# Six plain hidden tiles instead of four, two squares' sums moved between engines, and a later column sum

## The chip, the cores and the metric

One core of a Trainium2 chip runs the whole program. The metric is the device time of one execution in microseconds (us); a smaller number is better. The kernel before took 2752.27 us in the median of 3 runs (2752.18 to 2753.72).

## What is computed

Two stacks of two layers each, over 512 tokens of width 1024, in float32. The parts that the change touches are the two normalizations and the second stack's feed forward:

```python
def swiglu(h, w_gate_up, w_down):
    g, u = jnp.split(h @ w_gate_up, 2, axis=-1)      # hidden width 2816 = 22 tiles of 128
    return (jax.nn.silu(g) * u) @ w_down

# end of the first stack, then the start of the second
x = rmsnorm(x, norm_f)
h = rmsnorm_2(x, norm_mix_g[0])
...
mem_n = rmsnorm_2(mem, mem_norm_g[layer])            # mem: 256 tokens of width 1024
x = x + memory_cross_attention(rmsnorm_2(x, norm_xattn_g[layer]), mem_n, ...)
x = x + swiglu(rmsnorm_2(x, norm_ffn_g[layer]), ffn_w_gate_up[layer], ffn_w_down[layer])
```

## The kernel before

**Layout and arithmetic.** The state `x` stays in SBUF as 8 tiles of 128 features by 512 tokens. Every float32 matrix product is made of three matmuls (`mm3`, lines 225 to 227): each operand is split into a high and a low part, and high by high, high by low and low by high are summed in PSUM. Weights come by DMA on SP's queue (`_load`), are split by ScalarE (line 132) and VectorE (line 133), and at most `HL` = 4 split weight tiles are held ahead.

**Order of the work.** The program order on every engine is written out by hand. After each group of 24 matmuls, `tick` (line 200) does four things in this order: it splits weights for what comes next (`pump`), evacuates the PSUM result, runs what was put off, and lets each background generator do one step (`step`, line 177). So a generator advances one `yield` per tick, and what it issues stands in its engine's queue behind the weights and the evacuation of that tick.

**The second stack's feed forward** (`ffn`, line 1069, with `conv=False`; called twice). The 22 hidden tiles are taken in pairs, in the parts that `FPARTS` and `FPARTS_END` list (lines 437 and 438); after each part its down projection follows (`fd`). A pair is made in one of two ways:

- *plain*, for tiles below `PLAIN[1]`: two weight chunks `fa` and `fv`, 2 output tiles each, 8 features tiles deep, so 2 x 2 x 8 x 3 = 96 matmuls of 512 columns, on the input `xh`, `xl`. VectorE multiplies by `Rb` (line 1148), ScalarE applies Silu (line 1087), GpSimd multiplies by `Rb` again (line 1089), VectorE multiplies the two halves (line 1152), and ScalarE and VectorE split the result (lines 237 and 238).
- *by seven products* (`spair`, line 1092): the 2 by 2 block product is done with 7 block products instead of 8, each `product` (line 1054, matmul at line 1065) being 2 x 4 x 3 = 24 matmuls of 256 columns, so 168 for a pair. It needs sums of weight blocks (`schunks`, VectorE adds at line 327) and sums of blocks of the input, `self.A`.

`self.A` is made by the generator `factors` (line 995), which starts in the background after the first pair of `fa` tiles. It takes the 8 tiles of `x` two at a time (`j` = 0 to 3): one step computes `xa`, `xb` and four sums on VectorE (lines 1022 to 1028), the next step splits the sums of the pair before (`put`, ScalarE lines 1008 and 1011, VectorE lines 1009 and 1012). With the first step there are two steps per `j`, and the tenth step sets `self.ready`; four more steps make the factors `12` and `22`. Where the first pair by seven products begins, the code waits for it in program order:

```python
if f == plain:
    while not self.ready:
        self.step()
    self.xh = self.xl = None
```

The tiles of 128 x 512 come from one pool of `NT` = 45 buffers, beside 11 or 13 more for the factors (`ft`, line 1047).

**The end of the first stack.** `norm_tile` (line 543) splits each new tile of `x` and adds its squares up. Squares are made by ScalarE (lines 535 and 537). The running sums are kept by GpSimd for tiles 1 to 4 and by VectorE for tiles 5 to 7 (`dve`, line 547; the add is line 541). At the end of the first stack there are two sets of sums (`ngain2` is given there and nowhere else), since the final norm of the first stack and the first norm of the second are taken together. `even` (line 1294) then starts with `mem_k`: after its first 24 matmuls `norm_gen` (line 587) puts the column sums on TensorE (`colsum`, line 567, matmul at line 575).

**Memory's norm.** `mem_norm` (line 1226) is a generator in the background of the first stack's second feed forward. In one step it issues the squares of 8 tiles on ScalarE and 7 adds on GpSimd, then yields twice, then puts the column sum on TensorE.

Of the kernel before, what the change touches and what calls it, by code (L numbers as in the profile page):

```python
# [14 lines left out]
KT = 8  # L15
# [296 lines left out]
def wchunk(name, w, r0, kc, c0, nc_=256, split=whole):  # L312
    per = 1024 // nc_
    raws = [block(w, r0 + k * P, min(per, kc - k), c0, nc_) for k in range(0, kc, per)]
    return chunk(name, raws, [unit(r["kc"], nc_, split, (i,)) for i, r in enumerate(raws)])


def schunks(name, w, c1, c2):


    b = [block(w, r, 4, c, 256) for r, c in ((0, c1), (0, c2), (512, c2), (512, c1))]

    b11, b12, b22, b21 = b
    box = {}

    def add(c, to, x, y):
        c.nc.vector.tensor_tensor(to, x, y, op=ADD)

    def sum0(c, r):

        box["t"] = c.pf.tile([P, 1024], F32, tag="t0", bufs=1, name=c.nm("t0")).rearrange("p (k c) -> p k c", k=4)
        add(c, box["t"], r[0], r[1])

    def sum1(c, r):

        add(c, r[0], r[0], r[1])

    def sum2(c, r):

        add(c, r[0], r[0], r[1])  # L340

    def post5(c, r):

        add(c, r[0], r[0], r[1])

    def temp(c, hi, lo, raws):
        c.put(hi, lo, box.pop("t"))


    u = [dict(unit(4, 256, whole, (b11,), 0), pre=sum0, praws=(b11, b12)),  # L350
         dict(unit(4, 256, temp, (b11,), 0), pre=sum1, praws=(b12, b22)),
         dict(unit(4, 256, whole, (b11,), 0), pre=sum2, praws=(b11, b12)),
         unit(4, 256, whole, (b22,), 1),
         dict(unit(4, 256, whole, (b21, b11), 1, 1), post=post5, praws=(b21, b11)),
         unit(4, 256, whole, (b12,), 1),
         unit(4, 256, whole, (b21,), 1)]
    out = [chunk(name, [], [x]) for x in u]
    out[0]["raws"] = b
    return out
# [77 lines left out]
FPARTS = ((0, 6), (6, 12), (12, 16), (16, 22))  # L437
FPARTS_END = ((0, 6), (6, 12), (12, 18), (18, 22))

PLAIN = (22, 4)  # L440


def ffn_plan(wu, wd, b, end=False):
    pl, late, first = [], [], []
    pairs = {f: schunks("fs", wu, 2816 + 128 * f, 128 * f) for f in range(PLAIN[b], 22, 2)}
    parts = FPARTS_END if end else FPARTS
    for f0, f1 in parts:
        for f in range(f0, f1, 2):
            if f < PLAIN[b]:
                pl.append(wchunk("fa", wu, 0, 8, 128 * f))  # L450
# [13 lines left out]
        for i in range(2):  # L464
            for f in range(f0, f1, 2):
                pl.append(chunk("fd", [block(wd, 128 * f, 2, 512 * i, 512)], [unit(2, 512)]))
                if i == 0 and f == f0:
                    pl += late
                    late = []
                    if f1 - f0 == 4 and f1 >= PLAIN[b]:  # L470
                        first = pairs[f1][:1]
# [4 lines left out]
class Kern(Ctx):  # L476
# [66 lines left out]
    def norm_tile(self, j):  # L543

        g = self.ngain(j)
        self.xh[j], self.xl[j] = self.split(self.x[j], "x", scale=g)
        dve = j >= KT - 3
        self.sumsq(self.x[j], 0, dve=dve)
        if self.ngain2 is not None:
            self.sumsq(self.x[j], 1, scale=self.ngain2(j), dve=dve)  # L550
# [518 lines left out]
    def ffn(self, l, after, conv):  # L1069
# [3 lines left out]
        last = None  # L1073
        plain = PLAIN[0 if conv else 1]

# [150 lines left out]
    def mem_norm(self):  # L1226

        nc = self.nc
        mem = self.mem_load()
        for _ in range(6):  # L1230
            yield
        save, self.sqs = self.sqs, [[], []]
        for j in range(KT):
            self.sumsq(mem[:, j], 0)
        sq, self.sqs = self.sqs[0], save
        yield
        yield
        v = self.colsum(sq, 2, D)
        r = self.rsqrt(v, 2)
        yield  # L1240
        ps = self.rows(r, 2)
        self.mr = self.pc.tile([P, 2], F32, tag="mr", name="mr")
        nc.vector.tensor_copy(self.mr, r)
        self.mRb = self.pc.tile([P, 256], F32, tag="mRb", name="mRb")
        nc.scalar.copy(self.mRb, ps)
        yield from self.mem_split(0, mem)
# [876 lines left out]
```

## Time and profile before

| what | value |
| --- | --- |
| median of 3 runs | 2752.27 us |
| the profiled execution | 2754.49 us |
| its span, first to last instruction | 2752.5 us |
| mean granted TensorE clock in it | 0.990 |
| TensorE matmul busy | 2694.3 us (98%) |
| VectorE busy | 1652.9 us (60%) |
| ScalarE busy | 1106.1 us (40%) |
| GpSimd busy | 265.4 us (10%) |

The profiled execution is 2.2 us above the median. Matmul durations in the rows overlap each other (a row's 0.39 us is its latency), so a matmul's price is taken from start to start. PE is TensorE, DVE is VectorE, ACT is ScalarE, POOL is GpSimd; L575 is line 575. An arrow `<-` behind idle time names what ended it.

### The profile page before, as it was taken

What the parts mean: (1) busy time and instruction counts of PE and PEld (TensorE: products, weight loads), DVE (VectorE), ACT (ScalarE), POOL (GpSimd) and SP (SyncE); (2) the same over time, 40 slices, a digit from 0 to 9 for tenths busy, and PEclk for the clock granted to TensorE, in tenths of its full rate; (3) what the DMA queues carried; (4) which work ended last, traced back from release to release, by engine and by line L of the source; (5) the groups of instructions that cost most, each with busy time, mean ns of one, the idle gap of its engine ahead of it and who ended that gap; (6) DMA issues with size and microseconds to landing.
All of it is one profiled execution on the core that took longest, in us unless ns stands there. A gap on an engine that the chain in (4) does not pass through costs nothing.

```text
span 2752.5 us, 36388 instructions
## 1 busy us (share of the span) xinstructions
PE 2694.3 (98%) x14606; PEld 2307.3 (84%) x14606; DVE 1652.9 (60%) x2446; ACT 1106.1 (40%) x1668; POOL 265.4 (10%) x337
## 2 busy tenths in 40 slices
PE   8999999999999999999999998999999999989997
PEld 7888888888878888788888887899988888879997
DVE  5644654455455475555566567676766656677666
ACT  4353332233345334332343354443443535444334
POOL 1110200001011011010021201000011001100001
PEclk9999999999999999999999999999999999999999
DMA  5232323332323223332323332242232113223331
GB/s 190 62 93 77 92 92 100 101 99 92 115 63 93 73 89 100 108 100 85 104 81 119 108 99 66 86 127 94 89 93 84 54 47 107 92 77 108 93 100 54
DMA packets 236424, 254.77 MB, mean 93 GB/s; under 512 B 19904, under 2 KB 212672, under 8 KB 235616
## 3 DMA queue, kind: packets, MB, share of 16 engines
q1 hardware_dynamic: 233808, 245.70, 29.1%
q0 software_dynamic: 1440, 5.97, 0.6%
q8 instruction: 114, 1.87, 0.3%
q10 hardware_dynamic: 1008, 0.80, 0.1%
q14 instruction: 54, 0.44, 0.1%
HBM read 248.20 MB, written 2.10 MB: 91 GB/s over the span
## 4 chain that ended last, share of the span: by engine, by line
PE 91%; DVE 5%; ACT 2%; issue 1%; POOL 0%; DMA 0%; ACTq 0%; POOLq 0%; SPq 0%; DVEq 0%
PE ps L225 23%; PE ps L227 23%; PE ps L226 23%; PE ps L1065 13%; PE ps L964 1%; DVE lo L133 1%; PE ps L1740 1%; PE ps L800 1%; PE ps L575 1%; PE ps L1466 0%; PE ps L979 0%; PE ps L890 0%; PE ps L584 0%; ACT hi L132 0%; PE ps L1875 0%
## 5 line engine op out<-in xcount | busy, mean ns | idle before, releaser
L133 DVE TENSOR_TENSOR lo<-raw,hi 128x1024 fp32r<-128x1024 f32 (+3 forms) x519 | 610.3, 1201 | 268.4 <-ACT hi L132 265.4
L225 PE MATMUL ps<-xh,hi 128*128 128x512 f32 x1648 | 649.7, 394 | 7.7 <-ACT hi L132 7.7
L227 PE MATMUL ps<-xh,lo 128*128 128x512 f32 x1648 | 643.7, 391 | 0.7 <-DVE lo L133 0.7
L226 PE MATMUL ps<-xl,hi 128*128 128x512 f32 x1648 | 643.3, 390 | 0.0
L132 ACT ACTIVATE hi<-raw 128x1024 fp32r<-128x1024 f32 (+3 forms) x519 | 509.4, 1012 | 302.8 <-PE ps L226 236.2
L225 PEld LDWEIGHTS ps<-xh,hi 128*128 128x128 f32 x1648 | 310.6, 188 | 73.4 <-ACT hi L132 7.7
L227 PEld LDWEIGHTS ps<-xh,lo 128*128 128x128 f32 x1648 | 310.3, 188 | 67.2 <-DVE lo L133 1.9
L226 PEld LDWEIGHTS ps<-xl,hi 128*128 128x128 f32 x1648 | 310.7, 189 | 63.1 <-issue 0.2
L1065 PE MATMUL ps<-Ah,hi 128*128 128x256 f32 x1008 | 289.1, 287 | 14.1 <-ACT Ah L1008 13.1
L1065 PE MATMUL ps<-Al,hi 128*128 128x256 f32 x1008 | 288.4, 286 | 8.3 <-DVE Al L1009 8.3
L1065 PE MATMUL ps<-Ah,lo 128*128 128x256 f32 x1008 | 287.2, 285 | 0.0
L225 PE MATMUL ps<-acth,hi 128*128 128x512 f32 (+1 forms) x736 | 280.5, 381 | 2.2 <-ACT acth L237 2.2
L226 PE MATMUL ps<-actl,hi 128*128 128x512 f32 (+1 forms) x736 | 280.7, 381 | 0.6 <-DVE actl L238 0.6
L227 PE MATMUL ps<-acth,lo 128*128 128x512 f32 (+1 forms) x736 | 280.2, 381 | 0.0
L660 DVE TENSOR_TENSOR x<-ps,x 128x512 f32<-128x512 f32 x168 | 114.5, 687 | 161.4 <-PE ps L227 161.0
L1065 PEld LDWEIGHTS ps<-Ah,hi 128*128 128x128 f32 x1008 | 195.6, 194 | 16.8 <-ACT Ah L1008 13.9
L1065 PEld LDWEIGHTS ps<-Al,hi 128*128 128x128 f32 x1008 | 195.4, 194 | 10.5 <-DVE Al L1009 9.9
L1065 PEld LDWEIGHTS ps<-Ah,lo 128*128 128x128 f32 x1008 | 195.7, 194 | 0.0
L225 PEld LDWEIGHTS ps<-acth,hi 128*128 128x128 f32 x736 | 138.9, 189 | 28.6 <-ACT acth L237 2.6
L226 PEld LDWEIGHTS ps<-actl,hi 128*128 128x128 f32 x736 | 138.8, 189 | 27.0 <-DVE actl L238 1.3
L227 PEld LDWEIGHTS ps<-acth,lo 128*128 128x128 f32 x736 | 138.9, 189 | 26.4
L541 POOL TENSOR_TENSOR sq<-sq,sq 128x512 f32<-128x512 f32 (+1 forms) x53 | 69.6, 1319 | 695.5 <-ACT sq L535 695.0
(400 smaller groups left out, 3800.5 us busy)
## 6 DMA issues: line engine op xcount, KB each, us to landing
raw<-in_w_up SPq DMA_DIRECT2D x88, 512.0 KB, 3.7
raw<-in_ffn_w_gate_up SPq DMA_DIRECT2D x88, 512.0 KB, 3.6
raw<-in_w_in SPq DMA_DIRECT2D x78, 512.0 KB, 4.6
raw<-in_w_down SPq DMA_DIRECT2D x44, 512.0 KB, 4.3
raw<-in_ffn_w_down SPq DMA_DIRECT2D x44, 512.0 KB, 3.7
raw<-in_od_w_in SPq DMA_DIRECT2D x20, 512.0 KB, 3.8
raw<-in_w_o SPq DMA_DIRECT2D x16, 512.0 KB, 3.6
raw<-in_xattn_wkv SPq DMA_DIRECT2D x16, 512.0 KB, 4.6
```

Source lines behind the costliest of these rows:

```text
L132: self.nc.scalar.activation(hi, raw, AF.Copy)
L133: self.nc.vector.tensor_tensor(lo, raw, hi.bitcast(F32), op=SUB)
L225: mm(out, lhsT=wh, rhs=xh, start=first, stop=False)
L226: mm(out, lhsT=wh, rhs=xl, start=False, stop=False)
L227: mm(out, lhsT=wl, rhs=xh, start=False, stop=last)
L541: (nc.vector if dve else nc.gpsimd).tensor_tensor(acc[to], acc[to], q, op=ADD)
L575: nc.tensor.matmul(ps[:, i:i + 1], lhsT=q[:, t], rhs=self.ones[:, 0:1], start=(b == 0), stop=(b == len(sq) - 1))
L660: self.nc.vector.tensor_tensor(self.x[j], ps, self.x[j], op=ADD)
L800: nc.tensor.matmul(z[b][:, o:o + n], lhsT=k[rs, kt * P:(kt + 1) * P], rhs=q[rs, kt * P:S], start=(kt != 3), stop=False, skip_group_check=True)
L964: nc.tensor.matmul(o, lhsT=v, rhs=pt, start=not started[hh], stop=False, skip_group_check=True)
L1065: mm(o, lhsT=w, rhs=x, start=(first and nt == 0 and j == 0 and i == 0), stop=(j == 3 and i == 2), skip_group_check=True)
L1740: nc.tensor.matmul(z[b][:, o:o + n], lhsT=qT[h][:, T * P:(T + 1) * P], rhs=kT[h][:, 0:n], start=True, stop=True)
```

## The change

`PLAIN` says how many hidden tiles of a feed forward are plain, for the first and the second stack. The second entry goes from 4 to 6, so tiles 4 and 5 are made plain in both feed forwards of the second stack, and the part (0, 6) becomes all plain. Where two sets of squares are summed, VectorE adds only tile 7's, and GpSimd also tiles 5's and 6's. In `mem_norm` six yields stand between the squares and the column sum, instead of two.

```diff
-PLAIN = (22, 4)
+PLAIN = (22, 6)
@@ norm_tile
-        dve = j >= KT - 3
+        dve = j >= (KT - 3 if self.ngain2 is None else KT - 1)
         self.sumsq(self.x[j], 0, dve=dve)
         if self.ngain2 is not None:
             self.sumsq(self.x[j], 1, scale=self.ngain2(j), dve=dve)
@@ mem_norm
         for j in range(KT):
             self.sumsq(mem[:, j], 0)
         sq, self.sqs = self.sqs[0], save
-        yield
-        yield
+        for _ in range(6):
+            yield
         v = self.colsum(sq, 2, D)
```

## Rows read from the trace of the kernel before

**Rows 1.** Waits of TensorE over the whole run: us in total, times, longest.

```profile
PE ps L1065 <- ACT Ah L1008: 13.1, 2, 8.3
PE ps L1065 <- DVE Al L1009: 8.3, 5, 3.8
PE ps L575 <- DVE sq L541: 4.4, 1, 4.4
PE ps L575 <- POOL sq L541: 2.3, 1, 2.3
```

**Rows 2.** Windows, PE only: stretch in us, length, busy (matmuls), granted clock, DMA.

```profile
1426.13:1440.44 14.31, 9.92 (x48) 0.64 0.38 117
1711.07:1730.53 19.46, 6.78 (x27) 0.56 0.00 0
1679.10:1700.86 21.76, 21.76 (x97) 1.00 0.30 98
1780.37:1838.26 57.89, 57.89 (x481) 1.00 0.36 115
```

**Rows 3.** Timeline of PE around tile 4, both feed forwards: start, us, what.

```profile
1710.83 0.28 PE L1065 MATMUL ps<-Ah,hi 128*128 128x256 f32 x1
...
1719.64 0.58 PE L1065 MATMUL ps<-Ah,hi 128*128 128x256 f32 x1 [8.29 <-ACT Ah L1008]
...
1744.64 0.40 PE L225 MATMUL ps<-acth,hi 128*128 128x512 f32 x1
...
2417.32 0.28 PE L1065 MATMUL ps<-Ah,hi 128*128 128x256 f32 x1
...
2447.44 0.40 PE L225 MATMUL ps<-acth,hi 128*128 128x512 f32 x1
```

**Rows 4.** Timeline of DVE around tile 4, first of the two.

```profile
1707.89 1.21 DVE L327 TENSOR_TENSOR raw<-raw,raw 128x1024 f32<-128x1024 f32 x1
...
1713.61 0.74 DVE L1022 SCALAR_TENSOR_TENSOR xa<-x,prm,Rb 128x512 f32<-128x512 f32 x1
...
1717.90 0.69 DVE L238 TENSOR_TENSOR actl<-a,acth 128x512 fp32r<-128x512 f32 x1 [0.69 <-ACT acth L237]
...
1727.34 0.68 DVE L1012 SCALAR_TENSOR_TENSOR Al<-s,Ah 128x512 fp32r<-128x512 f32 x1
```

**Rows 5.** Windows, DVE only: stretch, length, busy (instructions), clock, DMA.

```profile
1677.00:1711.00 34.00, 28.37 (x39) 1.00 0.21 68
1711.00:1731.00 20.00, 16.08 (x30) 0.57 0.00 0
```

**Rows 6.** Timeline around memory's column sum, POOL and PE.

```profile
1096.55 7.71 POOL L541 TENSOR_TENSOR sq<-sq,sq 128x256 f32<-128x256 f32 x7
...
1101.58 0.39 PE L227 MATMUL ps<-xh,lo 128*128 128x512 f32 x1
1104.32 0.61 PE L575 MATMUL ps<-ones,sq 128*128 128x1 f32 x4 [2.35 <-POOL sq L541]
...
1109.44 0.40 PE L226 MATMUL ps<-xl,hi 128*128 128x512 f32 x1
```

**Rows 7.** Timeline at the end of the first stack, DVE, POOL and PE.

```profile
1408.52 0.75 DVE L241 SCALAR_TENSOR_TENSOR xl<-x,gfm,xh 128x512 fp32r<-128x512 f32 x1 [0.79 <-ACT xh L240]
...
1409.09 11.47 POOL L541 TENSOR_TENSOR sq<-sq,sq 128x512 f32<-128x512 f32 x8 [24.66 <-ACT sq L535]
...
1410.67 1.57 DVE L241 SCALAR_TENSOR_TENSOR xl<-x,gfm,xh 128x512 fp32r<-128x512 f32 x1 [0.79 <-ACT xh L240]
...
1421.04 1.28 DVE L541 TENSOR_TENSOR sq<-sq,sq 128x512 f32<-128x512 f32 x2
1422.24 2.35 DVE L133 TENSOR_TENSOR lo<-raw,hi 128x1024 fp32r<-128x1024 f32 x2
...
1430.80 3.58 PE L575 MATMUL ps<-ones,sq 128*128 128x1 f32 x16 [4.39 <-DVE sq L541]
```

**Rows 8.** Timeline of DVE later, in the second stack, beside a GpSimd multiply.

```profile
1505.74 3.48 DVE L133 TENSOR_TENSOR lo<-raw,hi 128x1024 fp32r<-128x1024 f32 x2
```

## The prediction

> **What bounds the kernel now.** I read the waits of TensorE first. In the whole run it waits long in few places [rows 1]: for the splits of the factors, 13.1 and 8.3 us (lines 1008 and 1009), and for two column sums, 4.4 us on VectorE's squares and 2.3 us on GpSimd's. Elsewhere the matmuls follow each other, so the time is the sum of TensorE's work and of these holes, and the change aims at all four of them.
>
> Then the windows, for what a matmul costs and for the clock. A stretch of plain work holds 96 matmuls of 512 columns in 21.76 us (the count of 97 has one that was in flight at its start), 226.7 ns each; a stretch of products holds 480 of 256 columns in 57.89 us, 120.6 ns each; both at a granted clock of 1.00, that is 2.4 GHz. In two of the holes it is lower [rows 2]: 0.64 around the norm at the end of the first stack and 0.56 at the first factor border. Those are stretches partly at 1.2 GHz, after TensorE had stood still. So a hole costs more than its wait, and I take each from start to start.
>
> Then the timeline around tile 4 [rows 3]. From the first product of the pair to the next down projection matmul it is 1744.64 - 1710.83 = 33.81 us in the first feed forward and 2447.44 - 2417.32 = 30.12 us in the second, for 6 products, 144 matmuls, worth 17.37 us at 120.6 ns. The holes are **16.4 and 12.8 us, 29.2 together**. VectorE tells why [rows 4]: at 1710.83 the factors of `j` = 2 and 3 were not begun (line 1022 at 1713.61), and their last split before the products ran at 1727.34. VectorE had been busy 28.4 of 34 us before that [rows 5], and ten steps at one per tick don't fit into the six ticks that two plain pairs give after the generator starts.
>
> **Tiles 4 and 5 plain.** Removed per feed forward: a pair of 168 matmuls, 20.26 us. Added: 96 matmuls, 21.76 us. That is +1.5 us twice, **+3.0 us** on TensorE, all on the path.
>
> The Trainium skill speaks against this part more strongly ("TensorE: Matmul & The Clock Gate", section "Back-to-back issue gap"): it gives a warm gap of columns / 2.4 plus 2.5 ns. By my estimate from it a plain pair would take 20.7 us and a seven-product pair 18.3 us, so two exchanges would cost 4.8 us and the time below would be 1.8 us later. The rows show 226.7 and 120.6 ns instead of 215.8 and 109.2, and I go by the rows.
>
> What it gives back: four more ticks before the border bring the steps to ten, exactly `ready`. And since the part (0, 6) is now all plain, its down projection follows before the first product: 144 matmuls of 512 columns, 32.6 us. So the factors are wanted 21.8 + 32.6 = 54.4 us later than now, and the last split ended 17 us after the border. The holes go: **-29.2 us**.
>
> What could be late next is VectorE. In the 20 us after the border it was busy 16.1 us [rows 5]: the rest of the factors and the evacuation of pair 2. The new pair adds six evacuating operations of about 0.69 us (line 238 in [rows 4]), 4.1 us, and four weight splits of 1.2 us (half of the 2.35 us for two in [rows 7]), 4.9 us; GpSimd's two multiplies by `Rb` can hold it up by some 2.6 us; three sums of weight blocks of 1.21 us [rows 4] move into the down projection, -3.6 us. That makes 24.1 us beside 21.8 us of plain matmuls: 2.3 us too much, if all of it had to be done by then. But only the split of the first down weights has to; the third pair's results are read by the last third of the first half, 10.9 us later, and the factors 32.6 us later. I take 0, and keep 2.3 us per feed forward as the other end. The weight bytes are the same for both kinds of pair, and SP's queue loads them in the same order apart from the down weights, which come before the next pair's; in these holes the DMA share was 0.00 [rows 2], so I cost the DMAs at nothing. Tile 6's pair begins behind a down projection in the kernel before too, and its products run on for 57.89 us without a hole [rows 2], so I expect none at that border.
>
> **Memory's column sum.** The last matmul before it starts at 1101.58, the first at full pace after it at 1109.44 [rows 6], with 13 matmuls of 512 columns between: 7.86 - 14 x 0.227 = 4.7 us, of which the column sum keeps 0.5. GpSimd's seven adds run from 1096.55 to 1104.26. Four more ticks are 4 x 24 x 0.227 = 21.8 us; the sum then comes 19 us after the adds' end: **-4.2 us**. The chain behind it moves as a whole, still tick by tick, in a stage of 22 plain tiles. If its next step waits as long as this one, the gain is 0.
>
> **Tiles 5 and 6 summed on GpSimd.** VectorE loses four adds, 2 x 1.28 us, of which the first two stand before two weight splits [rows 7]. GpSimd's eight adds took 11.47 us there, 1.3 to 1.7 us each, and while they ran VectorE's split of a new tile took 1.57 instead of 0.75 us: an operation with two SBUF inputs waits until the running GpSimd add has ended, and the next add waits for it. Two weight splits beside a single GpSimd multiply took 3.48 instead of 2.35 us [rows 8]. So tile 5's adds on GpSimd fall on the two weight splits and hold each up by about 1.2 us; with 1.28 us saved, tile 6 is about 1.2 us late; its own two adds gone, tile 7 is on time again; then tile 7's split waits for GpSimd's second add of tile 6, about 1 us, and the column sum starts **+0.9 us** later than at 1430.80. Bounds: -1.3 us if the two engines don't collide, +2.6 us if all four adds (1.3 us against 0.65) stand in a row on the path. A gain of 5 us is possible if TensorE waits shorter and its clock falls for less of this stretch (0.64 in [rows 2]).
>
> **The sum.** 3.0 - 29.2 - 4.2 + 0.9 = -29.5 us. Against the profiled execution's 2754.5 us that is 2725.0; it lay 2.2 us above the median, so against 2752.3 it is **2722.8 us**.
>
> **Rivals.** *VectorE becomes the bound in the plain stretch*: TensorE waits 2.3 us per feed forward for weights, and 0.8 us more for the slower pace behind a wait (the holes of 29.2 us hold 21.4 us of waits [rows 1], a third on top), 6.2 us in all: 2729.0 us. For it: 24.1 us of work beside 21.8. Against it: the order of need above, and that the second feed forward has no rope table to compute. *The column sum's wait comes back*, one step later in memory's chain, where VectorE's small operations queue: 4.2 us less gain, 2727.0 us. Against it: now no wait follows that step [rows 1]. *The end of the first stack gains*: GpSimd's adds run beside, and TensorE stays at 2.4 GHz for more of it: 5 us instead of +0.9, 2716.9 us. Against it: the 1.57 us.
>
> *Slower: the pool of 45 buffers.* With 16 tiles of `xh` and `xl`, 11 of results, 9 factors and 7 blocks of `x` and sums I count 43 at the ninth step. If it were over 45, the steps of `j` = 2 and 3 would wait for the end of the third plain pair, with the down weights' splits behind them on ScalarE and VectorE: 1727.3 - 1713.6 = 13.7 us of VectorE's queue [rows 4], 2.6 us for GpSimd's multiplies and 3.9 us for the pace behind a wait (half of 29.2 less 21.4), 20.2 us per feed forward where 14.6 stand now. Then 2 x 5.6 + 3.0 - 4.2 + 0.9 = +10.9, 2763.2 us. It decides from the 46th live buffer on; against it stands the count, and the other pool of 11 or 13. That an edit does nothing at all I can't see: each changes the order of the program.
>
> **Chances.** Forecast 0.62 (its own range 2719 to 2727), VectorE bound 0.15, wait comes back 0.07, more gain at the norm 0.13, buffers 0.03. A measurement of this kernel can tell 0.2%, 5.5 us, from no change. All cases but the last lie far beyond that; half of what I gain would have to fail for "same". The range 2716 to 2731 takes in the bounds of the norm, the clock and VectorE's 6.2 us, and leaves out the buffers and mixtures.
>
> **What would show it.** Right: no wait of line 1065 on lines 1008 and 1009; granted clock 1.00 from the start of both feed forwards to their third part; 896 matmuls of each of the three kinds at line 1065 (16 pairs of 56) where there were 1008; no wait of line 575 on GpSimd at memory's sum; the wait at the norm near 5 us, now partly on GpSimd. Wrong: waits of line 225 or 227 on lines 132 and 133 in the plain stretch, a wait of line 584 in memory's chain, or a product that still waits for its factors at tile 6.

## The result and the profile after

The kernel after takes 2723.1 us in the median of 4 runs (2721.69 to 2723.66), beside 2752.99 us of the kernel before in the same comparison (4 runs, 2752.18 to 2753.93): a ratio of 0.9891, 95% interval 0.9873 to 0.9908. The forecast was 2722.8 us. The profiled execution took 2723.18 us, its span is 2721.5 us and its mean granted clock 0.996, where it was 0.990.

The page, its part 1 (busy time, share, instructions) and one of the three groups of line 1065 (out<-in, count, busy us, mean ns, idle before):

```profile
PE 2685.9 (99%) x14462; PEld 2294.9 (84%) x14462; DVE 1636.9 (60%) x2418; ACT 1098.1 (40%) x1656; POOL 278.4 (10%) x345
...
L1065 PE MATMUL ps<-Ah,hi 128*128 128x256 f32 x896 | 254.6, 284 | 0.9 <-DVE a L1116 0.9
```

896 is the count that two pairs fewer give. TensorE's busy time fell by only 8.4 us (2694.3 us before), and its span by 31.0: the other 22.6 us were standing still. Busy time is not the amount of work either: a matmul that runs at 1.2 GHz counts longer (0.58 us for the one behind the wait in [rows 3], 0.28 for the others there), and the page before has more of these.

The waits of TensorE over the whole run, the four largest, to be laid beside [rows 1]:

```profile
PE ps L225 <- ACT hi L132: 8.2, 1, 8.2
PE ps L575 <- DVE sq L541: 4.6, 1, 4.6
PE ps L584 <- DVE ry L564: 3.9, 2, 2.4
PE ps L227 <- DVE lo L133: 2.7, 6, 0.7
```

The first is the start of the program and the third its end; both are in the kernel before too (7.7 and 3.9 us), where the prediction's "elsewhere the matmuls follow each other" passes over them. The two waits of line 1065 on lines 1008 and 1009 are gone, and so is that of line 575 on GpSimd. The norm's wait stands, at 4.6 us instead of 4.4.

Windows of TensorE: stretch, length, busy (matmuls), granted clock, DMA. The first is the whole first feed forward of the second stack, then its six plain tiles, their down projection, the plain tiles of the second feed forward, the stretch around memory's sum, and the norm:

```profile
1660.28:2013.74 353.46, 351.55 (x2178) 1.00 0.32 97
1673.35:1727.88 54.53, 54.53 (x244) 1.00 0.24 78
1727.88:1760.52 32.64, 32.64 (x146) 1.00 0.31 96
2364.91:2419.43 54.52, 54.52 (x243) 1.00 0.31 97
1095.00:1130.00 35.00, 35.00 (x160) 1.00 0.31 92
1421.80:1435.30 13.50, 8.88 (x44) 0.62 0.37 118
```

In the four rows in the middle busy time equals length: no hole is left. Where [rows 2] had a clock of 0.56 after the border it is 1.00. At the norm it is 0.62, as low as before (0.64). From first matmul to the first of the next stage, the first feed forward takes 353.5 us; in the kernel before it took 368.4, by this window:

```profile
1664.99:2033.43 368.44, 353.88 (x2250) 0.97 0.31 93
```

The second, from its first matmul to the last of the run, took 373.7 us and takes 362.4.

The timeline of TensorE at the border, the answer to [rows 3], first the end of the plain work, then the first product:

```profile
1727.88 0.39 PE L225 MATMUL ps<-acth,hi 128*128 128x512 f32 x1
...
1760.29 0.39 PE L227 MATMUL ps<-acth,lo 128*128 128x512 f32 x1
1760.52 0.28 PE L1065 MATMUL ps<-Ah,hi 128*128 128x256 f32 x1
```

The product follows the down projection after 0.23 us, the length of a matmul of 512 columns. On VectorE the factors end here, to be read against [rows 4]:

```profile
1725.16 2.35 DVE L133 TENSOR_TENSOR lo<-raw,hi 128x1024 fp32r<-128x1024 f32 x2
...
1730.41 0.69 DVE L1012 SCALAR_TENSOR_TENSOR Al<-s,Ah 128x512 fp32r<-128x512 f32 x1
```

The last split ends at 1731.10, 3.2 us after the plain matmuls and 29 us before the first product. The splits of the down weights (line 133) stand ahead of it, and TensorE did not wait for them. VectorE's windows over the plain tiles of both feed forwards:

```profile
1673.35:1727.88 54.53, 45.47 (x65) 1.00 0.24 78
2364.91:2419.43 54.52, 44.29 (x62) 1.00 0.31 97
```

Memory's column sum, on GpSimd and TensorE, the answer to [rows 6]:

```profile
1095.81 7.72 POOL L541 TENSOR_TENSOR sq<-sq,sq 128x256 f32<-128x256 f32 x7
...
1122.57 0.39 PE L227 MATMUL ps<-xh,lo 128*128 128x512 f32 x1
1122.79 0.50 PE L575 MATMUL ps<-ones,sq 128*128 128x1 f32 x4
1123.15 0.49 PE L225 MATMUL ps<-acth,hi 128*128 128x512 f32 x1
```

The adds end at 1103.5 and the sum comes 19 us later, without a wait on either side. The end of the first stack, on VectorE, GpSimd and TensorE, the answer to [rows 7]; line 660 is the add that makes a tile of `x`, here those of tiles 1, 6 and 7:

```profile
1402.05 0.68 DVE L660 TENSOR_TENSOR x<-ps,x 128x512 f32<-128x512 f32 x1
...
1404.10 15.41 POOL L541 TENSOR_TENSOR sq<-sq,sq 128x512 f32<-128x512 f32 x10 [24.66 <-ACT sq L535]
...
1416.65 3.94 DVE L133 TENSOR_TENSOR lo<-raw,hi 128x1024 fp32r<-128x1024 f32 x2 [0.52 <-ACT hi L132]
1420.52 0.68 DVE L660 TENSOR_TENSOR x<-ps,x 128x512 f32<-128x512 f32 x1
...
1422.61 2.90 POOL L541 TENSOR_TENSOR sq<-sq,sq 128x512 f32<-128x512 f32 x2 [3.10 <-ACT sq L535]
...
1424.68 1.38 DVE L241 SCALAR_TENSOR_TENSOR xl<-x,gfm,xh 128x512 fp32r<-128x512 f32 x1 [0.92 <-ACT xh L240]
1425.99 1.28 DVE L541 TENSOR_TENSOR sq<-sq,sq 128x512 f32<-128x512 f32 x2
1426.72 3.58 PE L575 MATMUL ps<-ones,sq 128*128 128x1 f32 x16 [4.62 <-DVE sq L541]
```

The two weight splits take 3.94 us, beside GpSimd's adds, and took 2.35 in [rows 7]. From tile 1's add to the column sum it is 1426.72 - 1402.05 = 24.67 us; in the kernel before it was 1430.80 - 1407.05 = 23.75, from the column sum in [rows 7] and this add:

```profile
1407.05 0.68 DVE L660 TENSOR_TENSOR x<-ps,x 128x512 f32<-128x512 f32 x1
```

### The profile page after: what moved, and what is told of

Its sections match the earlier page's. It is cut to its first block, busy times and chain, and to the rows that moved or that the text cites. A ratio compares the mean times of both kernels' runs of the same rounds, so it can differ in the third digit from the quotient of the medians.

```text
span 2721.5 us, 36076 instructions
## 1 busy us (share of the span) xinstructions
PE 2685.9 (99%) x14462; PEld 2294.9 (84%) x14462; DVE 1636.9 (60%) x2418; ACT 1098.1 (40%) x1656; POOL 278.4 (10%) x345
## 3 DMA queue, kind: packets, MB, share of 16 engines
q1 hardware_dynamic: 233808, 245.70, 29.5%
q0 software_dynamic: 1440, 5.97, 0.7%
q10 hardware_dynamic: 1008, 0.80, 0.1%
## 4 chain that ended last, share of the span: by engine, by line
PE 94%; DVE 3%; ACT 2%; issue 1%; POOL 0%; DMA 0%; ACTq 0%; POOLq 0%; SPq 0%; DVEq 0%
PE ps L225 25%; PE ps L227 25%; PE ps L226 25%; PE ps L1065 12%; PE ps L964 1%; PE ps L1740 1%; PE ps L800 1%; DVE lo L133 1%; PE ps L575 1%; PE ps L1466 1%; PE ps L979 0%; PE ps L890 0%; PE ps L584 0%; ACT hi L132 0%; PE ps L1875 0%
## 5 line engine op out<-in xcount | busy, mean ns | idle before, releaser
L133 DVE TENSOR_TENSOR lo<-raw,hi 128x1024 fp32r<-128x1024 f32 (+2 forms) x515 | 606.6, 1204 | 257.6 <-ACT hi L132 254.8
L225 PE MATMUL ps<-xh,hi 128*128 128x512 f32 x1712 | 673.2, 393 | 8.2 <-ACT hi L132 8.2
L227 PE MATMUL ps<-xh,lo 128*128 128x512 f32 x1712 | 667.4, 390 | 0.7 <-DVE lo L133 0.7
L226 PE MATMUL ps<-xl,hi 128*128 128x512 f32 x1712 | 667.1, 390 | 0.0
L132 ACT ACTIVATE hi<-raw 128x1024 fp32r<-128x1024 f32 (+2 forms) x515 | 505.1, 1013 | 293.5 <-PE ps L226 229.1
L1065 PE MATMUL ps<-Ah,hi 128*128 128x256 f32 x896 | 254.6, 284 | 0.9 <-DVE a L1116 0.9
L1065 PE MATMUL ps<-Al,hi 128*128 128x256 f32 x896 | 253.5, 283 | 0.0
L1065 PE MATMUL ps<-Ah,lo 128*128 128x256 f32 x896 | 253.5, 283 | 0.0
L1065 PEld LDWEIGHTS ps<-Ah,hi 128*128 128x128 f32 x896 | 171.8, 192 | 2.6 <-issue 1.1
L1065 PEld LDWEIGHTS ps<-Ah,lo 128*128 128x128 f32 x896 | 171.9, 192 | 0.0
L225 PEld LDWEIGHTS ps<-acth,hi 128*128 128x128 f32 x736 | 138.8, 189 | 28.7 <-ACT acth L237 2.6
```

The source lines that it names most:

```text
L132: self.nc.scalar.activation(hi, raw, AF.Copy)
L133: self.nc.vector.tensor_tensor(lo, raw, hi.bitcast(F32), op=SUB)
L225: mm(out, lhsT=wh, rhs=xh, start=first, stop=False)
L226: mm(out, lhsT=wh, rhs=xl, start=False, stop=False)
L227: mm(out, lhsT=wl, rhs=xh, start=False, stop=last)
L1065: mm(o, lhsT=w, rhs=x, start=(first and nt == 0 and j == 0 and i == 0), stop=(j == 3 and i == 2), skip_group_check=True)
```

## The experiments

The theory: the factors had too little time ahead of the first product, and the new pair with the down projection behind it gives that time; the exchange of the pairs costs some 1.5 us each, memory's sum brings some 4 us, and the squares cost about one. Against it stand: that the pace of one step per tick was the limit, not the amount of VectorE's work; that the down projection alone or the pair alone did it; that the exchange costs more than forecast; and that the squares' move was worth something. Each run stands beside runs of the kernel before on the same chip, which gave 2752.27 to 2753.03 us in the median.

### Each part alone

The first two experiments make one part of the change each on the kernel before, the third takes one part out of the kernel after.

```diff
 kernel before
-PLAIN = (22, 4)
+PLAIN = (22, 6)
```

> The kernel before with PLAIN = (22, 6) alone. My theory: the two factor holes go (29.2 us) and the two exchanged pairs cost 3.0 us, so 26.2 us less than the kernel before, about 2726.5 us; memory's column sum still waits 2.3 us and the norm at the end of the first stack 4.4 us. Rival (VectorE is the bound in the plain stretch): waits of lines 225 and 227 on lines 132 and 133 appear there, 6 us in all, about 2732 us.

```diff
 kernel before, mem_norm
-        yield
-        yield
+        for _ in range(6):
+            yield
```

> The kernel before with six yields ahead of memory's column sum, alone. My theory: 4.2 us less, about 2748.8 us, no wait of line 575 on GpSimd there and a granted clock of 1.00 through 1100 to 1130 us. Rival (the wait comes back one step later, at the row broadcast of line 584): no less time, 2753 us, with a wait of line 584 on line 564 near 1128 us.

```diff
 kernel after, norm_tile
-        dve = j >= (KT - 3 if self.ngain2 is None else KT - 1)
+        dve = j >= KT - 3
```

> The changed kernel with the squares of tiles 5 and 6 back on VectorE. My theory (GpSimd's adds and VectorE's operations with two SBUF inputs exclude each other): 0.9 us less than the changed kernel, about 2722.2 us; the column sum at the end of the first stack starts 0.9 us earlier after tile 1's add than it does there, and the two weight splits before tile 6 take 2.35 us again. Rival (the move relieves VectorE): 1 us more than the changed kernel, about 2724 us.

| kernel | median us (range) | ratio to before, 95% interval |
| --- | --- | --- |
| six plain tiles alone | 2726.34 (2725.98 to 2726.68) | 0.9901 (0.9886 to 0.9917) |
| memory's sum later alone | 2749.87 (2747.6 to 2750.4) | 0.9987 (0.9978 to 0.9996) |
| after, squares back on VectorE | 2721.25 (2719.36 to 2722.2) | 0.9882 (0.9869 to 0.9896) |
| kernel before, same comparison | 2752.94 (2750.93 to 2755.18) | |

The plain tiles alone bring 26.6 us, where 29.2 - 3.0 = 26.2 was forecast; the first feed forward takes 353.5 us, as in the kernel after. Memory's sum alone brings 3.1 us, with an interval of 1.1 to 6.1; in the trace its 35 us around the sum hold 159 matmuls at a clock of 1.00 where before the same 35 us held 141 at 0.95, and 18 matmuls of 0.227 us are 4.1 us. The window of the kernel before, then that of this one:

```profile
1095.00:1130.00 35.00, 32.65 (x141) 0.95 0.29 89
1095.00:1130.00 35.00, 35.00 (x159) 1.00 0.32 101
```

All traces of this document together say the same. Up to the add of tile 1 at the end of the first stack the code is the same in every kernel, apart from this edit; only the kernel with other parts, further below, differs there and is left out. The add comes at 1405.80 to 1407.05 us in the three traces without the edit and at 1401.06 to 1403.44 in the eight with it, 4.0 us earlier in the mean. The squares cost the kernel after 1.9 us; the ranges of the two kernels overlap (2719.36 to 2722.2 and 2721.69 to 2723.66), so that size is rough. The three add up to 26.6 + 3.1 - 1.9 = 27.8 us, against 29.9 together.

What the squares' move does is plainer in the trace of the third kernel than in its time. The end of the first stack, tile 1's add, the two weight splits and the column sum:

```profile
1402.44 0.68 DVE L660 TENSOR_TENSOR x<-ps,x 128x512 f32<-128x512 f32 x1
...
1417.63 2.35 DVE L133 TENSOR_TENSOR lo<-raw,hi 128x1024 fp32r<-128x1024 f32 x2
...
1426.18 3.44 PE L575 MATMUL ps<-ones,sq 128*128 128x1 f32 x16 [4.40 <-DVE sq L541]
```

With GpSimd's adds gone from that place the splits take 2.35 us again, and it is 23.74 us from the add to the sum, 0.93 less than in the kernel after. The other traces agree: 23.73 to 23.75 us in the five that have these adds on VectorE and the sum in its old place, 24.64 to 24.67 in the three that have them on GpSimd. From the sum on to the first feed forward the same traces differ by up to 1.5 us (232.7 to 234.2) whichever engine adds, so the 0.9 us is seen in this place and not beyond it.

### Twice the pace of the steps

```diff
 kernel before, four plain tiles kept
+    def twice(self, g):
+        for _ in g:
+            next(g, None)
+            yield
...
-                            gf = self.bg(self.factors())
+                            gf = self.bg(self.twice(self.factors()))
```

> The kernel before, four plain tiles, with the factor generator doing two of its steps per tick, so that its ten steps fit into the six ticks. If the pace of one step per tick made the holes, they go without the two exchanged pairs: 29 us less, about 2724 us. If VectorE's work made them (it was idle 5.6 of the 34 us before the first border), only some 6 us come back in the first feed forward and up to 12.8 in the second, which has no rope table: 6 to 19 us less, 2734 to 2747 us, and the products still wait on lines 1008 and 1009.

It took 2745.53 us (2744.36 to 2746.48), ratio 0.9972 (0.9962 to 0.9983): 7.4 us of the 29.2. Its lines lie 5 lower from here on, so line 1070 is the matmul of `product`. The waits of TensorE over the whole run:

```profile
PE ps L1070 <- ACT Ah L1008: 7.2, 2, 3.7
PE ps L1070 <- DVE lo L133: 6.3, 2, 3.8
```

And the windows of all engines: the end of the plain work, then from the first product to the next down projection matmul in both feed forwards; length, then busy time (instructions) of PE, PEld, DVE, ACT and POOL, granted clock, DMA:

```profile
1676.51:1710.64 34.13, 32.93 (x147) 26.93 (x145) 29.43 (x45) 14.39 (x23) 6.35 (x5) 1.00 0.21 62
1710.64:1740.11 29.47, 21.17 (x144) 20.18 (x145) 24.85 (x34) 14.72 (x22) 0.00 (x0) 0.83 0.20 65
2411.20:2438.23 27.03, 20.80 (x145) 20.01 (x144) 22.64 (x29) 12.26 (x19) 0.00 (x0) 0.81 0.23 72
```

The holes are 29.47 - 17.37 = 12.1 and 27.03 - 17.37 = 9.7 us, where they were 16.4 and 12.8: 4.3 and 3.1 us less, at the small end of what I expected for the case that VectorE's work makes them. VectorE is busy 29.4 of the 34.1 us ahead of the border and 24.9 of the 29.5 behind it, and half of TensorE's wait has only changed its name: the products now wait for weight splits (line 133) that queue behind the steps issued early. So the pace of one step per tick explains a quarter of the holes. That the rest is the amount of work that VectorE has to do before the border is argued from these busy times; no run takes work off VectorE there. If it is so, more of TensorE's work ahead of the border must help, and that the next two kernels try.

### The pair or the down projection

The kernel after gives both: 21.8 us of plain matmuls and 32.6 us of down projection. The next kernel keeps the pair and puts the down projection off, by a first part of eight tiles in the list that only the last feed forward uses:

```diff
 kernel after
-FPARTS_END = ((0, 6), (6, 12), (12, 18), (18, 22))
+FPARTS_END = ((0, 8), (8, 12), (12, 18), (18, 22))
```

> The changed kernel with the last feed forward's parts as (0, 8), (8, 12), (12, 18), (18, 22), so that tile 6's products follow the third plain pair with no down projection between. If the down projection's 32.6 us were part of what closes the holes, VectorE is late there: besides the factors (their last split ended 0.6 us before the plain tiles did) the three sums and first splits of the weight blocks, some 8 us, fall into the plain stretch, and a hole of 4 to 9 us opens at the first product, 2727 to 2732 us. Rival (the four ticks alone close them): no wait at that border, 2723 us.

It took 2726.1 us (2724.67 to 2727.72), ratio 0.9903 (0.9888 to 0.9918). I had expected 4 to 9 us of hole at the border. The edit leaves the first feed forward of the second stack as it is, with both; in the second this window (from the first product to the next down projection matmul) and this wait remain:

```profile
2417.39:2435.95 18.56, 17.79 (x146) 1.00 0.31 105
```

```profile
PE ps L1065 <- DVE Al L1009: 0.8, 2, 0.5
```

18.56 - 17.37 = 1.2 us. The expectation was wrong: the four ticks of the pair close the second feed forward's hole of 12.8 us almost alone. For the first, where the hole was 16.4 us and VectorE was later (below), the pair alone was not tried. The last feed forward is 3.5 us longer than in the kernel after (365.9 and 362.4): beside this 1.2 us, the part now cut to four tiles has a border of its own, where TensorE waits 1.65 us for line 237 and loses 2.4 from start to start.

The opposite kernel goes without the pair: four plain tiles, and their down projection right behind them. It stands on the version of the next section (squares back on VectorE, column sum two ticks later), which is its comparison; `FPARTS` serves the first stack too.

```diff
 kernel after, squares back, norm two ticks later
-FPARTS = ((0, 6), (6, 12), (12, 16), (16, 22))
-FPARTS_END = ((0, 6), (6, 12), (12, 18), (18, 22))
+FPARTS = ((0, 4), (4, 10), (10, 16), (16, 22))
+FPARTS_END = ((0, 4), (4, 12), (12, 18), (18, 22))
-PLAIN = (22, 6)
+PLAIN = (22, 4)
@@ ffn_plan
-                    if f1 - f0 == 4 and f1 >= PLAIN[b]:
+                    if f1 - f0 == 4 and f1 > PLAIN[b]:
@@ ffn
-                        if n == 4 and f1 >= plain:
+                        if n == 4 and f1 > plain:
```

> The run with the norm two ticks later and the squares back on VectorE, but with four plain tiles as before and the parts cut as (0, 4), (4, 10), (10, 16), (16, 22) and, in the last feed forward, (0, 4), (4, 12), (12, 18), (18, 22): the down projection of the four plain tiles (96 matmuls, 21.8 us) stands ahead of the first product. My theory (only the time between the generator's start and the first product counts, whatever fills it): the factors' last split ended 17.2 and 13.2 us after the border in the kernel before, so at most a small hole is left, up to 3 us with the sums of the weight blocks; the two exchanged pairs' 2.5 us come back, and the hole of about 2 us behind the four-tile part at tile 12 goes too. 2 to 5 us less than the run with both, 2712 to 2715 us. Rival (the ticks of the fifth and sixth plain tile are needed, since VectorE evacuates and splits for the down projection meanwhile): waits of line 1065 on lines 1008 and 1009 are back, more than 8 us, 2722 us or more.

It took 2716.35 us (2715.89 to 2719.84), beside 2716.93 (2716.3 to 2718.44) of its comparison: no difference that these runs can tell. From the first product to the next down projection matmul, both feed forwards:

```profile
1725.19:1785.58 60.39, 58.66 (x481) 1.00 0.36 112
2413.69:2491.90 78.21, 78.21 (x650) 1.00 0.37 113
```

480 matmuls of the products are worth 57.9 us, so a hole of 2.5 us is left in the first feed forward, and 648 are worth 78.1 us, so none in the second. The waits in that hole, 1.7 us together, are for the evacuation of the products (lines 1099, 1103 and 1110) and not for the factors. The two feed forwards are 1.4 and 1.6 us shorter than in the comparison (350.47 and 360.85 us against 351.85 and 362.45). In the second that is about what a pair by seven products saves; in the first it is a sum of three things: that saving of 1.3 us, the new hole of 2.5, and the border behind the four-tile part at tile 12, 2.4 us in the comparison, which is gone. A new wait of 1.2 us (line 584 on line 564) stands in memory's chain in the first stack. I had expected 2 to 5 us less than the comparison, and that was wrong. What the two kernels show is that some 21.8 us more of TensorE's work ahead of the first product is nearly enough, the pair (in the second feed forward) or the down projection (in both); the kernel after has both, and more than it needs.

### One pair more

```diff
 kernel after
-PLAIN = (22, 6)
+PLAIN = (22, 8)
```

> The changed kernel with PLAIN = (22, 8): one more pair made plain in each feed forward. My theory, by the price of 1.5 us for an exchange and with no hole left to close: 3.0 us more than the changed kernel, about 2726.1 us. By the skill's page on TensorE (columns / 2.4 plus 2.5 ns) it would be 4.8 us more, 2727.9 us. Rival (seven products bring VectorE more work than plain tiles, and something is gained from less of it): 2723 us or less.

It measures the price of an exchange with no hole beside it. The median is 2727.11 us (2724.08 to 2727.69), 4.0 above the kernel after with a spread of 3.6, which does not tell an exchange of 1.5 us from one of 2.4, so I take the traces: the first feed forward is 354.74 us (353.46 after), the second 363.56 (362.36). The first of them:

```profile
1662.29:2017.03 354.74, 352.83 (x2106) 1.00 0.31 97
```

An exchange costs **1.3 and 1.2 us**. Another 2.0 us between the two profiled executions lie ahead of the first feed forward, which begins at 1662.29 and 1660.28 us, and there the two kernels have the same code. The forecast took 1.5 from rows of one stretch each. The Trainium skill's gap of columns / 2.4 plus 2.5 ns ("TensorE: Matmul & The Clock Gate", section "Back-to-back issue gap"), which that section gives for a matmul by itself and not for a stream of weight loads and matmuls, would make it 2.4 by my estimate; these traces do not bear that out.

### The column sum two ticks later

```diff
 kernel after, even
-        gn = self.bg(self.norm_gen())
+        def late():
+            for _ in range(2):
+                yield
+            yield from self.norm_gen()
+        gn = self.bg(late())
```

> The changed kernel with the norm's column sum at the start of the second stack two ticks later (two yields ahead of the norm's generator). My theory: the column sum then stands behind 48 more matmuls of 256 columns, 5.8 us, which is more than the 4.8 us that TensorE stood still; the wait goes, the granted clock stays at 1.00, and the stretch gives back most of the 10 us that it loses, 7 to 9 us less than the changed kernel, about 2715 us. Rival (the chain behind the sum is VectorE's and the wait comes back at the row broadcast of line 584, or at the first matmuls that need the rows): 0 to 3 us less, 2720 to 2723 us.

A second kernel, run on two occasions, also has the squares back on VectorE.

```diff
 kernel after with the edit above, norm_tile
-        dve = j >= (KT - 3 if self.ngain2 is None else KT - 1)
+        dve = j >= KT - 3
```

> The same with the squares of tiles 5 and 6 back on VectorE. My theory: once the column sum waits for nothing, it no longer matters which engine adds them; the time is that of the run with the norm two ticks later, within 0.5 us, about 2715 us. Rival (GpSimd's adds also delay the split of the new tiles, which is on the path): 1 us less than that run.

> The run with the norm two ticks later and the squares back on VectorE once more, beside the run with other parts on the same chip: 2716.8 us within 1 us by any theory.

The first took 2718.17 us (2717.99 to 2718.28), ratio 0.9874 (0.9858 to 0.9891), 4.9 us below the kernel after where I expected 7 to 9; with the squares back it is 2716.84 (2716.17 to 2717.95), and 2716.93 (2716.3 to 2718.44) in the repetition, ratio 0.9869 (0.9854 to 0.9884). That is 1.3 us below the first, where I had expected no more than 0.5: the rival's 1 us is nearer, and from tile 1's add to the first feed forward the traces give 254.6 us for the first and 253.9 for the second, twice. With the squares back it is the best version here, 6 us below the kernel after; the one with four plain tiles equals it. The waits of TensorE from 1405 to 1450 us in the first of them:

```profile
PE ps L227 <- DVE lo L133: 2.3, 3, 1.3
PE ps L225 <- ACT hi L132: 1.7, 1, 1.7
```

The column sum waits for nothing now. What is late next are the splits of `mem_k`'s second weight chunk, which stand behind tile 7's norm on ScalarE and VectorE; the granted clock from 1421.82 to 1440 us is 0.91 where the kernel after has 0.72. And not all of the gain is of this place. From tile 1's add to the first feed forward the traces give 3.6 us (258.2 and 254.6); another 1.7 us between the two profiled executions are the clock at a border further on, told of below.

## Why the prediction was right

**The holes, -29.2, and the exchange, +3.0.** Together they were to give 14.9 us in the first feed forward and 11.3 in the second; the traces give 368.4 - 353.5 = 14.9 and 373.7 - 362.4 = 11.3 (both come without the rest of the change too: 353.5 and 362.3 us with the plain tiles alone). The exchange is a little cheaper than taken, 2.5 us for both instead of 3.0, so the holes gave back some 28.7 of their 29.2 us, and two small errors cancel. Taking a hole from start to start, and not by its wait, is what made the sum come out: the waits of line 1065 were 21.4 us.

**The reason for the holes** was told less well. "Ten steps at one per tick don't fit into the six ticks" names the pace, and the doubled pace gave back 7.4 us only. The other half of that reading, VectorE busy 28.4 of 34 us, fits the runs better: with more of TensorE's work ahead of the first product the holes close, and with more steps per tick they do not. The 54.4 us that the factors were given are some 30 more than they needed, as the last split shows (1731.10, wanted at 1760.52) and as the two kernels with one cover each confirm, the one without the down projection for the second feed forward alone.

**VectorE's shortfall.** The estimate of 2.3 us beyond the plain matmuls came out at 3.2 in the first feed forward and, with no rope table, at -0.6 in the second (its last split ends at 2418.81, the plain work at 2419.43). Taken as 0 it was right, for the reason given: in neither stretch does a matmul wait for lines 132 or 133. That answers the rival of VectorE as the bound, at 45.5 us busy of 54.5.

**Memory's sum, -4.2.** 18 matmuls more in the same 35 us, 4.1 us; 4.0 by when the first stack ends in eleven traces; and by the medians 3.1, with an interval that holds 4.2. No wait of line 584 followed in the kernel after, so the rival of the wait that comes back fell; that it is near shows in the kernel with other parts, where 1.2 us of it appear.

**The squares, +0.9.** 24.67 - 23.75 = 0.92 us, and step by step as forecast: against tile 1's add, tile 6's add is 1.0 us later than before (18.47 against 17.46 us), tile 7's on time within 0.2 (21.03 against 20.80), and its split ends 0.9 late. Two operations that meet on the two engines take turns: the weight splits 3.94 instead of 2.35 us, a tile's split 1.56 instead of 0.75. The Trainium skill has this rule ("SBUF — State Buffer", section "Who interferes with whom"): a VectorE operation with two inputs in SBUF and a GpSimd operation that reads SBUF exclude each other for a whole instruction. The trace agrees. The rival that GpSimd's adds run beside and bring 5 us is thereby refuted; the part of the change that moves them costs 0.9 us where the column sum starts and 1.9 by the medians.

**The buffers.** No wait points to a pool run dry, and the kernel is faster; a run with fewer buffers was not tried, so at which count they would decide stays open.

One line of "what would show it" was not borne out: the wait at the norm is released by VectorE's adds alone, not by GpSimd's. The granted clock is 1.00 up to the third part in both feed forwards, as told; what happens at the third part in the first stands in the last section.

The time itself, 0.3 us off, owes something to luck: the parts measured alone add up to 27.8 us, the forecast's to 29.5, the whole to 29.9, and single executions of the kernel after spread over 2.0 us.

## What to carry to other kernels

A hole's price is read from the start of the stretch to the start of the next, with the work in it taken off at the price of a row at full clock; the waits alone gave 21 of 29 us here. When background work is late, ask whether its pace or its amount is the limit: a faster pace only lets it push other work back on the same engine, while a pair more of plain matmuls in front of it, with its down projection behind, cost 1.3 us a feed forward and closed holes of 16.4 and 12.8. Before sums are moved to GpSimd to unload VectorE, look at which VectorE operations with two SBUF inputs they will fall on.

## What was not expected of the hardware

In the down projection of the third part (tiles 12 to 15) of the first feed forward, TensorE waits 1.66 us for line 237. In the kernel after, what follows runs slower for a while; the timeline of TensorE there:

```profile
1904.59 0.50 PE L225 MATMUL ps<-acth,hi 128*128 128x512 f32 x1 [1.66 <-ACT acth L237]
...
1905.89 0.52 PE L225 MATMUL ps<-acth,hi 128*128 128x512 f32 x1
...
1909.54 0.39 PE L225 MATMUL ps<-acth,hi 128*128 128x512 f32 x1
```

and the window between the last two of these:

```profile
1905.89:1909.54 3.65, 3.65 (x10) 0.53 0.02 4
```

Nine matmuls in 3.65 us, most of it at 1.2 GHz. The kernel without a down projection between has the same code as the kernel after up to the last feed forward, instruction by instruction. In its trace the same wait ends at the same instruction, and the same nine matmuls take 2.04 us at 2.4 GHz; the timeline and the window:

```profile
1904.24 0.50 PE L225 MATMUL ps<-acth,hi 128*128 128x512 f32 x1 [1.65 <-ACT acth L237]
...
1905.54 0.39 PE L225 MATMUL ps<-acth,hi 128*128 128x512 f32 x1
...
1907.58 0.39 PE L225 MATMUL ps<-acth,hi 128*128 128x512 f32 x1
```

```profile
1905.54:1907.58 2.04, 2.04 (x10) 1.00 0.03 8
```

The difference, 1.6 us, is nearly that of the whole feed forward in these two traces (353.46 and 351.74 us). So the code does not decide it alone: the same code ran either way in two executions. Of the other profiled executions, those of the kernel before, of each part alone (the plain tiles, memory's sum), of the kernel after with only the squares back and of one pair more show a stretch at 1.2 GHz there; those of twice the pace and of the three runs with the later column sum and the parts uncut do not. What decides it no run here shows. It means that some 1.6 us can come or go at a wait with no change of code, and that differences of 1 to 2 us in the medians above are to be read with the traces beside them.
